# Feed-forward up-projection by seven quarter products, with buffers per sub-layer and the modulation sums moved

## The chip, the cores and the metric

The kernel runs on one core of a Trainium2 chip. The engines of a core each work through a queue of their own in order: TensorE (PE in the profile) multiplies matrices, VectorE (DVE), ScalarE (ACT) and GpSimd (POOL) work elementwise, and SyncE (SP) starts DMA transfers. They wait for one another through semaphores. The metric is the device time of one execution in microseconds (us).

## The reference

Two layers of a diffusion backbone run on 640 tokens (512 latent and 128 context) of 1024 channels. Each layer has a token mixer and then a feed-forward. Only the second is computed in another way by the change:

```python
def conv_glu(h, w_up, conv, w_down):
    u, val = jnp.split(h @ w_up, 2, axis=-1)     # 1024 -> 2 x 2816
    u = dwconv3(u, conv)                         # width 3, along the tokens
    return (jax.nn.gelu(u, approximate=True) * val) @ w_down

h = rmsnorm(x, g2n) * (1 + sc2) + sh2
x = x + gt2 * conv_glu(h, w_up, f_conv, w_down)
```

Shifts, scales and gates (`sh1, sc1, gt1, sh2, sc2, gt2`) come from `silu(c) @ w_mod + b_mod`, once for the latent tokens and once for the context tokens: 48 columns of 128 channels per layer.

## The kernel before

All matrices are float32. A product is made from three float32r products: weights and activations are each split into a high and a low part (`split`, L148 to L150, and in `block`, L127 and L128: ScalarE casts the high part, VectorE subtracts it to get the low part), and `gemm` (L136 to L147) sums high x high, high x low and low x high in PSUM. Channels lie on partitions. The 640 tokens are two halves of 320 columns (256 latent, 64 context), and a product tile of 128 channels is a pair of PSUM banks, one half in each. There are three such pairs (`mmps`, L102 to L109). A block of weights is 128 x 1024 (8 tiles of 128 channels) and needs 8 x 3 x 2 = 48 matmuls of 128x320.

`layer` (L648) runs a layer: norm, queries, keys and values, attention, pooling and short convolution, three branch projections (`branch`, 8 slots each, 24 in all), the output projection (`project`), the second norm (`norm`, one half of the tokens at a time, all from ready buffers) and `feed_forward` (L591). There, each of 22 channel tiles `f` has a gate block and a value block: 96 matmuls. ScalarE evacuates the gate product (L608), the convolution runs on ScalarE and VectorE (L293 to L295), ScalarE applies the GELU (L610), VectorE multiplies by the value product (L616) and the result is split. `PARTS` cuts the 22 tiles into two parts of 11; after each part `project` adds its share of the down-projection to `x`.

The modulation sums (`mod_block`, L162: two DMAs, four accumulating VectorE instructions and a small one for each of the 48 columns) are put behind other work by `aside`: in layer 0 one per branch slot (24), and two per tile of layer 0's feed-forward for the other 56.

Work is recorded in program order per engine and then ordered by a scheduler that sets each engine's queue and inserts the semaphore waits. All SBUF tiles come from pools that live for the whole kernel, so that the weights of the next stage can be fetched while the last one still runs.

Of the kernel before, what the change touches and what calls it, by code (L numbers as in the profile page):

```python
# [16 lines left out]
P = 128  # L17
D = 1024
# [19 lines left out]
KSPARE = (4, 4, 3)  # L38
FTAGS = [("yc", 8)] + [("g", 2)] * 2 + [("vm", 9)] * 9 + [("qk", 10)] * 10
# [6 lines left out]
PARTS = ((0, 11), (11, 22))  # L46
KSPLIT = (6, 5)
# [7 lines left out]
def hybrid_kernel(ctx: ExitStack, tc: tile.TileContext, a):  # L55
# [3 lines left out]
    wp = ctx.enter_context(tc.tile_pool(name="wp", bufs=1))  # L59
    act = ctx.enter_context(tc.tile_pool(name="act", bufs=1))  # L60
# [22 lines left out]

    count = [0]
# [3 lines left out]
    fturn = [0]  # L88
# [5 lines left out]

    def big(tag, bufs, dt=F32):
        return act.tile([P, N], dt, tag=tag, bufs=bufs, name=uid(tag))

    def tmp(dt=F32, width=N):
        t = act.tile([P, PPW], dt, tag="tmp", bufs=NTMP, name=uid("tmp"))
# [14 lines left out]
    def block(src, n=1024, spare=None):  # L114
        """spare: places (first column, end, tag and bufs of both parts) for when the rotating ones are all held."""
        raw = wp.tile([P, 1024], F32, tag="raw", bufs=NRAW, name=uid("raw"))
        nc.sync.dma_start(raw[:, :n], src)
        parts = []
        if spare is None:
            hi = wp.tile([P, 1024], F32R, tag="hi", bufs=NW, name=uid("hi"))  # L120
            lo = wp.tile([P, 1024], F32R, tag="lo", bufs=NW, name=uid("lo"))
            parts.append((0, n, hi, lo))
# [39 lines left out]
    def mod_block(l, i, cond):  # L162
        acc = sm.tile([P, 2, 2], F32, tag="macc", name=uid("macc"))
        for hf in range(2):
            turn[0] += 1
            tag, w = (("pt", 768), ("kc", 512), ("pt", 768), ("vca", 512))[turn[0] % 4]
            raw = act.tile([P, w], F32, tag=tag, bufs=2 if tag == "pt" else 1, name=uid("mraw"))[:, :512]
            nc.sync.dma_start(raw, a["w_mod"][l, i, :, hf * 512:(hf + 1) * 512])
            for s in range(2):
                scr = big("yt", 1)  # L170
# [25 lines left out]
    def rsqrt(st, v, r, t):  # L196
        """r = 1 / sqrt(st / D + EPS), with a Newton step"""
# [7 lines left out]
    def rstd(x, c, n=1):  # L205
        """1 / rms of the tokens of n halves from c on, the same on all partitions: one PSUM bank per half."""
# [17 lines left out]
    def half_tiles(n=2):  # L224
        t = act.tile([P, 768], F32, tag="pt", bufs=2, name=uid("xr"))
# [43 lines left out]
    def leading(n, src, h):  # L269
        """The first products after a norm: each half of the tokens for n blocks before the next half."""  # L270
# [95 lines left out]
    def softmax(s_ps, w, bias):  # L366
        s = act.tile([P, 384], F32, tag="s", bufs=4, name=uid("s"))
# [13 lines left out]
    def attention(l, qs, ks, vb, vc):  # L381
        kc = act.tile([P, 512], F32, tag="kc", bufs=1, name=uid("kc"))
        nc.sync.dma_start(kc, a["kc"][l].rearrange("p t n -> p (t n)"))
        vca = act.tile([P, 512], F32, tag="vca", bufs=1, name=uid("vca"))
# [4 lines left out]
        def behind(ins):  # L389
            """The products with V of the unit before: TensorE comes to them a little later than they could start."""  # L390
# [494 lines left out]
```

## Time and profile before

| | |
|---|---|
| three timed runs | 2156.16 us median (2154.4 to 2160.48) |
| span of the profiled execution | 2153.5 us (the page gives this execution by its span alone) |
| TensorE busy | 2114.8 us, 98% |
| VectorE busy | 1116.8 us, 52% |
| ScalarE busy | 723.3 us, 34% |
| GpSimd busy | 100.6 us, 5% |
| share of TensorE in the chain that ended last | 93% |
| HBM read | 216.10 MB, 103 GB/s over the span |

Busy times of TensorE include the overlap of pipelined matmuls: a matmul of 128x320 is shown with 310 ns, while the next one starts some 147 ns later. The granted TensorE clock is 1.00 (2.4 GHz) in nearly the whole span, and 0.50 (1.2 GHz) in a stretch near the start.

### The profile page before, as it was taken

The page shows a single profiled execution, that of the slowest core. Times are in us where ns is not written, and L with a number is a line of the kernel's source. Part 1 is how long each engine was busy: PE and PEld are TensorE (multiplying, and loading weights), DVE is VectorE, ACT ScalarE, POOL GpSimd, SP SyncE. Part 2 cuts the span into 40 slices and gives each one's busy share as a digit, 9 for nine tenths or more (in the row PEclk, how much of TensorE's full clock was granted, in tenths as well). Part 3 has the DMA queues.
Part 4 walks back from the last instruction along what each step waited for, and adds up shares of the span by engine and source line. Part 5 has one row for each costly group of instructions (what it writes and reads, how often), then busy time and mean ns, then how long its engine had stood idle before and what let it go on. Part 6 is the DMA issues. An engine that isn't in the chain of part 4 may idle for free.

```text
span 2153.5 us, 34873 instructions
## 1 busy us (share of the span) xinstructions
PE 2114.8 (98%) x14280; PEld 2038.5 (95%) x14280; DVE 1116.8 (52%) x2265; ACT 723.3 (34%) x1194; POOL 100.6 (5%) x300
## 2 busy tenths in 40 slices
PE   6999999999999999999999999999999999999998
PEld 4977999999999999999998779999999999999997
DVE  4247555556568778786352565323344643334434
ACT  4235432222354321333242452322223533123321
POOL 1001000000020000000020100000000200000000
PEclk9999999999999999999999999999999999999999
DMA  8241323345424445453322312222233222222222
GB/s 299 74 127 51 111 90 128 118 128 153 142 78 157 151 135 187 155 159 118 128 72 81 117 51 92 73 73 75 91 100 95 69 70 64 83 89 69 70 61 76
DMA packets 92032, 229.38 MB, mean 107 GB/s; under 512 B 10593, under 2 KB 20321, under 8 KB 91873
## 3 DMA queue, kind: packets, MB, share of 16 engines
q1 hardware_dynamic: 91872, 227.16, 33.4%
q8 instruction: 112, 1.84, 0.3%
q14 instruction: 48, 0.39, 0.1%
HBM read 216.10 MB, written 6.29 MB: 103 GB/s over the span
## 4 chain that ended last, share of the span: by engine, by line
PE 93%; DVE 3%; ACT 1%; POOL 1%; DMA 1%; issue 0%; SPq 0%; DVEq 0%; ACTq 0%; POOLq 0%
PE mm L141 60%; PE m L141 25%; PE ps L411 1%; PE ps L422 1%; PE m L401 1%; DVE h L150 1%; PE mm L346 1%; PE mm L344 1%; PE mm L345 1%; PE mm L732 1%; POOL xr L237 1%; POOL xr L234 0%; PE m L405 0%; DVE lo L128 0%; ACT h L149 0%
## 5 line engine op out<-in xcount | busy, mean ns | idle before, releaser
L141 PE MATMUL mm<-h,hi 128*128 128x320 f32 x3648 | 575.0, 310 | 1.0 <-ACT h L149 0.5
L141 PEld LDWEIGHTS mm<-h,hi 128*128 128x128 f32 x3648 | 542.2, 188 | 8.4 <-issue 2.1
L128 DVE TENSOR_TENSOR lo<-raw,hi 128x1024 fp32r<-128x1024 f32 (+1 forms) x240 | 278.8, 1162 | 367.8 <-PE mm L141 173.3
L127 ACT CAST hi<-raw 128x1024 fp32r<-128x1024 f32 (+1 forms) x240 | 240.5, 1003 | 585.0 <-PE mm L141 363.2
L141 PE MATMUL mm<-h,lo 128*128 128x320 f32 x1824 | 294.5, 310 | 0.0
L141 PEld LDWEIGHTS mm<-h,lo 128*128 128x128 f32 x1824 | 272.8, 188 | 3.4 <-issue 1.4
L171 DVE SCALAR_TENSOR_TENSOR yt<-mraw,cond 128x512 f32<-128x512 f32 x320 | 219.9, 687 | 5.4
L141 PE MATMUL m<-h,hi 128*128 128x320 f32 x1152 | 183.4, 311 | 4.1 <-ACT h L149 3.8
L141 PEld LDWEIGHTS m<-h,hi 128*128 128x128 f32 x1152 | 172.1, 188 | 8.7 <-ACT h L149 5.8
L128 DVE TENSOR_TENSOR yc<-raw,yc 128x512 fp32r<-128x512 f32 (+3 forms) x98 | 61.0, 624 | 130.0 <-ACT yc L127 72.8
L141 PE MATMUL mm<-vm,hi 128*128 128x320 f32 x626 | 113.1, 309 | 0.0
L141 PE MATMUL mm<-h,yc 128*128 128x320 f32 x672 | 100.9, 309 | 0.5 <-ACT tmp L608 0.5
L141 PE MATMUL m<-h,yc 128*128 128x320 f32 x672 | 100.9, 309 | 0.0
L141 PEld LDWEIGHTS mm<-h,yc 128*128 128x128 f32 x672 | 99.1, 188 | 0.7 <-ACT tmp L608 0.7
L141 PEld LDWEIGHTS m<-h,yc 128*128 128x128 f32 x672 | 99.1, 188 | 0.3 <-ACT tmp L608 0.3
L141 PEld LDWEIGHTS mm<-vm,hi 128*128 128x128 f32 x626 | 97.2, 188 | 0.4 <-DVE vm L150 0.4
L127 ACT CAST yc<-raw 128x512 fp32r<-128x512 f32 (+3 forms) x98 | 53.2, 565 | 130.0 <-DMA raw<-in_w_down 86.1
L141 PE MATMUL m<-h,lo 128*128 128x320 f32 x576 | 90.6, 308 | 0.0
L141 PEld LDWEIGHTS m<-h,lo 128*128 128x128 f32 x576 | 86.1, 188 | 0.0
L141 PE MATMUL mm<-yc,hi 128*128 128x320 f32 x370 | 75.4, 309 | 0.0
L141 PE MATMUL mm<-qk,hi 128*128 128x320 f32 x436 | 68.6, 309 | 0.0
L141 PEld LDWEIGHTS mm<-qk,hi 128*128 128x128 f32 x436 | 65.1, 188 | 0.0
(240 smaller groups left out, 2675.6 us busy)
## 6 DMA issues: line engine op xcount, KB each, us to landing
raw<-in_w_in SPq DMA_DIRECT2D x96, 512.0 KB, 3.6
raw<-in_w_up SPq DMA_DIRECT2D x88, 512.0 KB, 3.6
mraw<-in_w_mod SPq DMA_DIRECT2D x160, 256.0 KB, 2.9
raw<-in_w_branch SPq DMA_DIRECT2D x24, 512.0 KB, 3.5
raw<-in_w_down SPq DMA_DIRECT2D x30, 384.0 KB, 3.1
raw<-in_w_down SPq DMA_DIRECT2D x30, 320.0 KB, 2.9
raw<-in_w_out SPq DMA_DIRECT2D x16, 512.0 KB, 3.6
bm<-in_bias SPq DMA_DIRECT2D x16, 384.0 KB, 4.0
```

The costliest lines, as they stand in the source:

```text
L127: nc.scalar.copy(hi[:, :c1 - c0], raw[:, c0:c1])
L128: lows[0] = nc.vector.tensor_tensor(lo[:, :c1 - c0], raw[:, c0:c1], hi[:, :c1 - c0].bitcast(F32), ALU.subtract)
L141: nc.tensor.matmul(ps[:, c, :HALF], lhsT=w, rhs=v[:, c * HALF:(c + 1) * HALF], start=first, stop=last)
L150: return nc.vector.tensor_tensor(lo, src, hi.bitcast(F32), ALU.subtract)
L171: nc.vector.scalar_tensor_tensor(scr[:, :512], raw, 1.0, cond[s][:, hf * 512:(hf + 1) * 512], ALU.mult, ALU.mult, accum_out=acc[:, s, hf:h ...
L237: nc.gpsimd.tensor_scalar(t[:, HL:], t[:, HL:], sc[:, 1:2], sh[:, 1:2], ALU.mult, ALU.add)
L344: nc.tensor.matmul(o, lhsT=xh[:, tok], rhs=wh, start=(k == 0), stop=False)
L345: nc.tensor.matmul(o, lhsT=xh[:, tok], rhs=wl, start=False, stop=False)
L346: nc.tensor.matmul(o, lhsT=xl[:, tok], rhs=wh, start=False, stop=(k == KD - 1))
L401: nc.tensor.matmul(sps[:, e, 0:256].rearrange("p (r c) -> p r c", c=32), lhsT=qs[t][hs, j * P:(j + 1) * P], rhs=kb, start=True, stop=True)
L411: ins = nc.tensor.transpose(tp[:, b * P:(b + 1) * P], s[:, b * P:(b + 1) * P], ident)
L422: nc.tensor.matmul(y[e * 64:e * 64 + 64, 0:P], lhsT=v[:, t * P + e * 64:t * P + e * 64 + 64], rhs=pt[:, b, e, :], start=(b == 0), stop=(b ...
```

## The change

The two halves of the tokens and the two halves of the input channels make a 2 x 2 grid of `x`; gate and value columns with the two halves of the input channels make a 2 x 2 grid of the weights. Each tile `f` is then computed by seven products of sums of quarters (`seven`), each 12 matmuls of 128x320, or 84 for a tile. The sums of weight quarters are made on VectorE for each tile (`sums_block`), the sums of the norm's output once per sub-layer (`norm_quarters`). The first two products of a pair of banks start it, the later ones add to what the bank holds, and between them the bank is read: by ScalarE into a copy (`snap`) or by VectorE (`gate`, `val1`, `val0`). The gate product's evacuation moves to VectorE as the sum of the bank and a copy. The feed-forward has three parts (8, 8 and 6 tiles) instead of two.

SBUF tiles other than `x` and a few others now come from a pool per sub-layer (`Stage`), whose memory the next sub-layer's pool takes over. All modulation sums run in the branch slots: in layer 0 two per slot (48), in layer 1 up to two (32). The diff, cut to its core:

```diff
-PARTS = ((0, 11), (11, 22))
+PARTS = ((0, 8), (8, 16), (16, 22))
...
+    class Stage:
+        def __init__(self, name):
+            self.name = name
+            self.guard = tc.tile_pool(name=uid(name), bufs=1, reuse_waits="tile")
...
-                aside(ins, side, 1)
+                aside(ins, side, (len(side) + 23 - left[0]) // (24 - left[0]))
+                left[0] += 1
...
+    def split_quarters(out, t, ps):
+        n = 512 * len(ps)
+        hi, lo = own([P, 1024], F32R, "hi", 3, "hi"), own([P, 1024], F32R, "lo", 3, "lo")
+        split(t, hi[:, :n], lo[:, :n])
+        for j, p in enumerate(ps):
+            out[p] = (hi[:, j * 512:(j + 1) * 512], lo[:, j * 512:(j + 1) * 512])
+    def sums_block(raw, out):
+        if not out:
+            split_quarters(out, raw[:, 0:1024], (2, 1))
+        q = [raw[:, i * 512:(i + 1) * 512] for i in range(4)]
+        st = own([P, 2048], F32, "st", 1, "st")
+        s4, s3, s1, s2 = (st[:, i * 512:(i + 1) * 512] for i in range(4))
+        nc.vector.tensor_tensor(st[:, 512:1536].rearrange("p (b n) -> p b n", b=2),
+                                raw[:, 512:1536].rearrange("p (b n) -> p b n", b=2),
+                                q[3].unsqueeze(1).to_broadcast([P, 2, 512]), ALU.add)
+        nc.vector.tensor_tensor(s2, s1, q[1], ALU.add)
+        nc.vector.tensor_tensor(s4, s2, q[0], ALU.add)
+        for t, ps in ((st[:, 1024:2048], (5, 6)), (st[:, 0:1024], (3, 7)), (q[2], (4,))):
+            split_quarters(out, t, ps)
+        return out
+    def snap(src):
+        t = short("sn")
+        nc.scalar.copy(t, src)
+        return t
+    def seven(w, xt, ps, c11, c22, c12, c21):
+        a_, c_ = ps[:, 0, :HALF], ps[:, 1, :HALF]
+        kept = {}
+        def product(p, o, fresh):
+            for j, (wi, xi) in enumerate(((0, 0), (1, 0), (0, 1))):
+                for k in range(NP):
+                    nc.tensor.matmul(o, lhsT=w[p][wi][:, k * P:(k + 1) * P], rhs=xt[k][p][xi],
+                                     start=fresh and j == 0 and k == 0, stop=j == 2 and k == NP - 1,
+                                     skip_group_check=not fresh)
+        def one():
+            product(1, a_, True)
+            kept[1] = snap(a_)
+        def two():
+            product(2, c_, True)
+            c11(c_, kept[1])
+        def six():
+            product(6, a_, False)
+            kept[2] = snap(a_)
+        def five():
+            product(5, c_, True)
+            kept[5] = snap(c_)
+        def sev():
+            product(7, a_, False)
+            c22(a_, kept[5])
+        def three():
+            product(3, c_, False)
+            c12(c_, kept[2])
+        def four():
+            product(4, a_, False)
+            c21(a_)
+        return [one, two, six, five, sev, three, four]
...
+            nc.vector.tensor_tensor(x7, b22, b12, ALU.subtract)
+            nc.vector.scalar_tensor_tensor(x6, x7, -1.0, b11, ALU.mult, ALU.subtract)
+            two(u, i, 7, 6)
...
+                nc.vector.tensor_tensor(x5, b11, b12, ALU.subtract)
+                nc.vector.scalar_tensor_tensor(x4, x6, -1.0, b21, ALU.mult, ALU.subtract)
+                two(v, i, 5, 4)
...
+            def gate(c):
+                def do(psum, s):
+                    for (o, n), at in (((0, HL), LAT0 + c * HL), ((HL, HC), CTX0 + c * HC)):
+                        nc.vector.tensor_tensor(u[:, at:at + n], psum[:, o:o + n], s[:, o:o + n], ALU.add)
+                return do
+            def val1(psum, s):
+                got["v"] = short("v")
+                nc.vector.scalar_tensor_tensor(got["v"], psum, -1.0, s, ALU.mult, ALU.subtract)
+            def val0(psum):
+                cv = dwconv(u, "ffn_conv", l, f, KF)
+                nc.scalar.activation(cv[:, 1:PADW - 1], cv[:, 1:PADW - 1], AF.Gelu_apprx_tanh)
+                y = tmp()
+                for (o, n), at in (((0, HL), LAT0), ((HL, HC), CTX0)):
+                    nc.vector.scalar_tensor_tensor(y[:, o:o + n], psum[:, o:o + n], -1.0, cv[:, at:at + n],
+                                                   ALU.mult, ALU.mult)
+                for (o, n), at in (((0, HL), LAT0 + HL), ((HL, HC), CTX0 + HC)):
+                    nc.vector.tensor_tensor(y[:, HALF + o:HALF + o + n], got["v"][:, o:o + n], cv[:, at:at + n], ALU.mult)
+                got["y"] = y
+            return seven(w, xt, mmps(), gate(0), val1, gate(1), val0), got
```

In `up`, `gate(c)` is two VectorE sums from PSUM (256 and 64 columns, L752), `val1` one (320 columns, L757), and `val0` the convolution, the GELU and four VectorE products (L764, L767).

**TensorE, a tile of the feed-forward.** Before, in layer 1, a gate and a value block and the start of the next tile; `mm` and `m` are pairs of banks, `h` the norm's output, `hi`, `lo` and `yc` parts of the weights. Left out are rows without a wait.

```order
L141 MATMUL mm_17795<-h_16467,hi_17791 128x320 [waits DVE_49,PE_49,Activation_49]
...
L141 MATMUL mm_17795<-h_16467,lo_17792 128x320 [waits DVE_49]
...
L141 MATMUL mm_17861<-h_16467,hi_17857 128x320 [waits PE_49,Activation_49]
...
L141 MATMUL mm_17861<-h_16467,lo_17858 128x320 [waits DVE_49]
...
L141 MATMUL m_2785_17927<-h_16467,yc_17919 128x320 [waits DVE_49,PE_49]
```

Now, in layer 0, one tile (`mm_8158`) and the start of the next (`m_1427_8296`); `hT` are quarters of the norm's output and their sums. The rows shown start products 2, 6, 5 and 7, then product 1 of the next tile, its low part, products 3 and 4, and product 2 of the next tile.

```order
L653 MATMUL mm_8158<-hT_6301,hi_8134 128x320 [waits Activation_49]
...
L653 MATMUL mm_8158<-hT_6349,hi_8142 128x320 [waits DVE_49]
...
L653 MATMUL mm_8158<-hT_6370,hi_8142 128x320 [waits Activation_49]
...
L653 MATMUL mm_8158<-hT_6349,hi_8146 128x320 [waits Activation_49]
...
L653 MATMUL m_1427_8296<-hT_6301,hi_8272 128x320 [waits PE_49,Activation_49]
...
L653 MATMUL m_1427_8296<-hT_6301,lo_8273 128x320 [waits DVE_49]
...
L653 MATMUL mm_8158<-hT_6374,hi_8146 128x320 [waits DVE_49]
...
L653 MATMUL mm_8158<-hT_6370,hi_8150 128x320 [waits DVE_49]
...
L653 MATMUL m_1427_8296<-hT_6301,hi_8272 128x320 [waits Activation_49]
```

A block had waits at its start and at its low part. Now each product has one at its start: products 6, 3 and 4 for VectorE (by the semaphore counts for the end of `gate(0)`, `val1` and `gate(1)`), products 2, 5 and 7 for ScalarE (the three `snap`s). Each time that is the instruction which reads the product just before it, in the other bank of the pair. Product 1 of the next tile stands around product 3.

**VectorE, from one tile to the next.** Before, in the feed-forward of layer 1: `lo` and `yc` are weight parts for later blocks, `tmp` the convolution and the product, `vm`, `qk` the result's low part.

```order
L128 TENSOR_TENSOR lo_17598<-raw_17595,hi_17597 128x1024
L294 SCALAR_TENSOR_TENSOR tmp_17458<-tmp_17452,vecs,tmp_17458 128x642
L295 SCALAR_TENSOR_TENSOR tmp_17458<-tmp_17452,vecs,tmp_17458 128x642
L616 TENSOR_TENSOR tmp_17518<-mm_17469,tmp_17458 128x2x256
L616 TENSOR_TENSOR tmp_17518<-mm_17469,tmp_17458 128x2x64
L128 TENSOR_TENSOR lo_17660<-raw_17657,hi_17659 128x1024
L150 TENSOR_TENSOR qk_17522<-tmp_17518,qk_17521 128x640
L128 TENSOR_TENSOR yc_17728<-raw_17723,yc_17727 128x512
L128 TENSOR_TENSOR yc_17920<-raw_17917,yc_17919 128x512
L294 SCALAR_TENSOR_TENSOR tmp_17590<-tmp_17584,vecs,tmp_17590 128x642
```

Now, in layer 0, from the low part of products 5 and 6's weights for the next tile (`lo_8281`) to the end of that tile's `gate(0)` (both rows of `tmp_8292`):

```order
L171 TENSOR_TENSOR lo_8281<-st_8276,hi_8280 128x1024 [waits Activation_49]
L315 SCALAR_TENSOR_TENSOR tmp_8255<-tmp_8154,vecs,tmp_8255 128x642 [waits Activation_49]
L316 SCALAR_TENSOR_TENSOR tmp_8255<-tmp_8154,vecs,tmp_8255 128x642 [waits DVE_49,Pool_49]
L171 TENSOR_TENSOR lo_8285<-st_8276,hi_8284 128x1024 [waits Activation_49]
L764 SCALAR_TENSOR_TENSOR tmp_8260<-mm_8158,tmp_8255 128x256 [waits PE_49,Activation_49]
L764 SCALAR_TENSOR_TENSOR tmp_8260<-mm_8158,tmp_8255 128x64
L767 TENSOR_TENSOR tmp_8260<-v_8227,tmp_8255 128x256
L767 TENSOR_TENSOR tmp_8260<-v_8227,tmp_8255 128x64
L171 TENSOR_TENSOR lo_8289<-raw_8269,hi_8288 128x512 [waits Activation_49]
L752 TENSOR_TENSOR tmp_8292<-m_1427_8296,sn_8309 128x256 [waits PE_49]
L171 TENSOR_TENSOR gs_8266<-tmp_8260,gs_8265 128x640 [waits Activation_49]
L752 TENSOR_TENSOR tmp_8292<-m_1427_8296,sn_8309 128x64
```

The two L315 and L316 rows are the convolution, L764 and L767 `val0`, `gs_8266` the low part of the finished tile. The next tile's `gate(0)` has come to stand behind the convolution, two low parts of weights, `val0` and the low part of the result, and it is itself cut in two by the last of these.

**ScalarE at the same place, now.** `hi_8272`, `hi_8280`, `hi_8284` and `hi_8288` are the four high parts of the next tile's weights, `sn` the copies of banks, `tmp_8255` the convolution's middle tap and then the GELU.

```order
L170 CAST hi_8272<-raw_8269 128x1024 [waits DMAHW2_49,Activation_49]
L170 CAST hi_8280<-st_8276 128x1024 [waits DVE_49,PE_49,Activation_49]
L314 ACTIVATE tmp_8255<-tmp_8154,vecs 128x642 [waits DVE_49,Pool_49]
L641 COPY sn_8309<-m_1427_8296 128x320 [waits PE_49]
L170 CAST hi_8284<-st_8276 128x1024 [waits PE_49,Activation_49]
L761 ACTIVATE tmp_8255<-tmp_8255 128x642 [waits DVE_49]
L170 CAST hi_8288<-raw_8269 128x512 [waits DMAHW3_49,PE_49,Activation_49]
L170 CAST gs_8265<-tmp_8260 128x640 [waits DVE_49]
L641 COPY sn_8337<-m_1427_8296 128x320 [waits DVE_49,PE_49]
```

The three buffers of `hi` go round: `hi_8280` waits for TensorE to end product 3 of the tile before, `hi_8284` for product 4, and `hi_8288` for product 2 of its own tile. Before, the high parts had waits of the same kind, on blocks that had been multiplied earlier.

## Rows read from the trace of the kernel before

**Rows 1.** The page's busy times: engine, us, share of span, instructions.

```profile
PE 2114.8 (98%) x14280; PEld 2038.5 (95%) x14280; DVE 1116.8 (52%) x2265; ACT 723.3 (34%) x1194; POOL 100.6 (5%) x300
```

**Rows 2.** Busy time by stretch; the first row names the columns.

```profile
core 0: us, PE busy (x) PEld busy (x) DVE busy (x) ACT busy (x) POOL busy (x), PEclk, DMA share, GB/s
320.00:592.00 272.00, 272.00 (x1855) 271.81 (x1854) 160.83 (x317) 74.37 (x86) 0.00 (x0) 1.00 0.42 132
610.00:640.00 30.00, 28.31 (x179) 25.48 (x178) 23.03 (x55) 17.55 (x35) 14.14 (x27) 1.00 0.17 53
640.00:1086.00 446.00, 445.55 (x3038) 444.89 (x3038) 327.50 (x776) 143.02 (x225) 8.08 (x67) 1.00 0.46 146
1370.00:1640.00 270.00, 270.00 (x1841) 269.81 (x1841) 89.54 (x97) 71.24 (x83) 0.00 (x0) 1.00 0.28 85
1688.00:2136.00 448.00, 448.00 (x3055) 447.37 (x3055) 174.28 (x257) 144.42 (x226) 3.30 (x60) 1.00 0.23 71
```

**Rows 3.** The chain that ended last, inside the first feed-forward: start, us, what.

```profile
694.82 14.08 PE mm L141 x96
```

**Rows 4.** VectorE by line, operation and shape: count, busy us, mean ns, idle before.

```profile
L128 DVE TENSOR_TENSOR lo<-raw,hi 128x1024 fp32r<-128x1024 f32 x198 | 241.4, 1220 | 319.8 <-PE mm L141 142.4 <-PE m L141 70.5 <-issue 56.7
L128 DVE TENSOR_TENSOR yc<-raw,yc 128x512 fp32r<-128x512 f32 x78 | 53.6, 690 | 109.5 <-ACT yc L127 72.8 <-PE mm L141 14.2 <-ACT hi L127 10.1
L295 DVE SCALAR_TENSOR_TENSOR tmp<-tmp,vecs,tmp 128x642 f32<-128x642 f32 x52 | 47.6, 916 | 2.2
L294 DVE SCALAR_TENSOR_TENSOR tmp<-tmp,vecs,tmp 128x642 f32<-128x642 f32 x52 | 45.9, 884 | 15.9 <-ACT tmp L293 15.7
L230 DVE TENSOR_TENSOR xr<-ps,mx 128x320 f32<-128x320 f32 x48 | 22.1, 480 | 0.7 <-PE ps L219 0.6
L150 DVE TENSOR_TENSOR vm<-tmp,vm 128x640 fp32r<-128x640 f32 x24 | 19.7, 820 | 4.6 <-ACT vm L149 4.6
L616 DVE TENSOR_TENSOR tmp<-mm,tmp 128x512 f32<-128x512 f32 x30 | 20.7, 689 | 66.7 <-PE mm L141 66.7
L616 DVE TENSOR_TENSOR tmp<-mm,tmp 128x128 f32<-128x128 f32 x30 | 8.4, 280 | 0.0
L562 DVE SCALAR_TENSOR_TENSOR mx<-mm,mod,mx 128x256 f32<-128x256 f32 x14 | 6.7, 481 | 11.4 <-PE mm L141 11.3
L562 DVE SCALAR_TENSOR_TENSOR mx<-mm,mod,mx 128x64 f32<-128x64 f32 x14 | 3.8, 274 | 0.0
```

**Rows 5.** ScalarE in the same view.

```profile
L127 ACT CAST hi<-raw 128x1024 fp32r<-128x1024 f32 x198 | 207.6, 1050 | 511.9 <-PE mm L141 320.0 <-PE m L141 140.5 <-PE mm L346 18.1
L127 ACT CAST yc<-raw 128x512 fp32r<-128x512 f32 x78 | 46.7, 617 | 122.4 <-DMA raw<-in_w_down 86.1 <-DMA raw<-in_w_up 34.9 <-PE mm L141 1.3
L293 ACT ACTIVATE tmp<-tmp,vecs 128x642 f32<-128x642 f32 x52 | 43.3, 833 | 16.4 <-DVE tmp L476 11.2 <-issue 2.2
L610 ACT ACTIVATE tmp<-tmp 128x642 f32<-128x642 f32 x44 | 32.6, 741 | 89.6 <-DVE tmp L295 89.6
L608 ACT COPY tmp<-mm 128x512 f32<-128x512 f32 x28 | 16.4, 588 | 50.6 <-PE mm L141 50.5
L608 ACT COPY tmp<-mm 128x128 f32<-128x128 f32 x28 | 7.6, 271 | 0.0
```

**Rows 6.** The timeline of a branch slot: start, us, engine, what, idle before.

```profile
340.75 2.36 PE L141 MATMUL mm<-h,lo 128*128 128x320 f32 x15
343.14 0.71 ACT L540 ACTIVATE g<-mm 128x640 f32<-128x640 f32 x1 [1.29 <-PE mm L141]
```

**Rows 7.** Busy time by stretch near the start; columns as in Rows 2.

```profile
28.00:32.00 4.00, 1.26 (x6) 0.61 (x5) 2.77 (x4) 2.83 (x6) 0.00 (x0) 0.97 1.05 386
32.00:36.00 4.00, 4.00 (x17) 4.00 (x18) 4.00 (x9) 0.58 (x1) 0.52 (x1) 0.50 1.05 388
36.00:40.00 4.00, 4.00 (x21) 4.00 (x21) 1.85 (x4) 1.69 (x3) 2.42 (x3) 0.67 1.04 406
56.00:60.00 4.00, 2.37 (x16) 2.11 (x15) 4.00 (x2) 0.00 (x0) 2.72 (x2) 1.00 0.00 0
```

More of the change, by code (lines that the diff above doesn't have):

```diff
@@ L87, in hybrid_kernel @@
     busy = [False]
-    fturn = [0]
     lows = [None]
@@ L119, in block @@
         if spare is None:
[L120 to L122 removed]
+            parts.append((0, n, own([P, 1024], F32R, "hi", NW, "hi"), own([P, 1024], F32R, "lo", NW, "lo")))
         else:
@@ L526, in aside, with branch @@
         del side[:n]
-    def branch(l, b, h, ys, merged, last=False, side=[], between=None):
+    def branch(l, b, h, ys, merged, left, last=False, side=[], between=None):
         parts = []
@@ L570, in project @@
             gemm(ps, get(m), xt)
-            aside(residual(l, x, ps, m, part), side, 2)
+            aside(residual(l, x, ps, m, part), side, 1)
         if n_last:
@@ L620, in feed_forward @@
-                gs.append((gh, gl))
-                aside(ins, side, 2 if f < f1 - 1 else 0)
-            def wdown(m, i=0):
-                out = []
-                k0 = f0
-                spare = iter([("yc", 8)] * 6)
-                for n in KSPARE if i else KSPLIT:
-                    places = [(0, n * P, next(spare), next(spare))] if i else None
-                    src = a["w_down"][l, m, :, k0 * P:(k0 + n) * P]
-                    blk = block(src, n * P, places) if f1 == KF and m >= KD - 2 else ffn_block(src, n * P)
-                    out += [cols(blk, k) for k in range(n)]
-                    k0 += n
-                return out
@@ L635, in feed_forward @@
-            assert f1 < KF or not side
-            rb = project(l, x, wdown, 5, gs, 2 if f1 == KF else 0, side)
+                    steps, got = lead[f]
+                    sums_block(raws[0] if f == 0 else load_quarters(a["w_up"][l, f]), ws[f])
+                else:
+                    steps, got = up(f)
+                for step in steps:
+                    step()
+                gs.append(finish(got))
+            n = f1 - f0
+            last = f1 == KF
+            raws = {}
+            def wdown(m, i=0):
+                if m % 2 == 0 or not raws:
+                    raws["t"] = own([P, 2048], F32, "raw", 2, "raw")
+                raw = raws["t"][:, m % 2 * 1024:m % 2 * 1024 + n * P]
+                nc.sync.dma_start(raw, a["w_down"][l, m, :, f0 * P:f1 * P])
+                hi, lo = own([P, 1024], F32R, "hi", 3, "hi"), own([P, 1024], F32R, "lo", 3, "lo")
+                split(raw, hi[:, :n * P], lo[:, :n * P])
+                return [cols([(0, n * P, hi, lo)], k) for k in range(n)]
@@ L637, in feed_forward @@
+            rb = project(l, x, wdown, 5, gs, 2 if last else 0)
         return rb
@@ L646, in mods, with mixer @@
         return [do(i) for i in idx]
-    def layer(l, x, rb):
+    def mixer(l, x, rb):
         if l == 0:
```

200 lines of the change are left out of this document (129 added, 71 removed).

## The prediction

> **What bounds the kernel now.** I read the page's busy times first: TensorE works 98% of the span, the others half of it or less [rows 1]. Then the busy times by stretch: in both feed-forwards (640 to 1086 us, 1688 to 2136 us) and in the branch stages TensorE has no gap, while VectorE is 73% busy in layer 0's feed-forward, which carries modulation sums, and 39% in layer 1's, which carries none [rows 2]. So TensorE's matmuls set the end, and their price is their spacing. The chain of waits shows 96 of them in 14.08 us, 0.1467 us each [rows 3]: a tile of the feed-forward (a gate and a value block) takes 14.08 us.
>
> **What the change removes.** A tile needs 84 matmuls instead of 96. Over 22 tiles and 2 layers that is 528 x 0.1467 = 77.4 us less. If TensorE stayed without gaps, a tile would take 12.32 us.
>
> **What it adds to a tile.** TensorE will not stay without gaps. In the built order each product has a wait at its start for the instruction that reads the product before it, although that one lies in the other bank of the pair. So the products of a tile do not run beside their evacuations; they alternate with them. The only other work for TensorE is product 1 of the next tile around product 3, and product 2 after product 4. I follow one tile round, from the start of product 6 to that of the next tile's.
>
> A product takes 11 x 0.147 plus 0.31 for its last matmul (the last of 15 in 2.36 us [rows 6]), 1.92 us. A `snap` of 320 columns lies between the PSUM copies of 128 and 512 columns, 0.271 and 0.588 us: 0.43 [rows 5]. `val1` is like a VectorE operation on 320 columns from PSUM, 0.48; `gate` has 256 and 64 columns, by the line through 0.280 (128) and 0.689 (512) 0.416 and 0.212; `val0` has two scalar operations (0.481, 0.274) and two plain ones (0.416, 0.212), 1.38 [rows 4].
>
> - From product 6 to the end of product 3: product 6 1.92, snap 0.43, product 5 1.92, snap 0.43. ScalarE then casts the next tile's first high part (1.05), VectorE makes its low part (1.22) and only then `val1` (0.48), which is queued behind it; product 7 (1.92) runs beside the first two of these. Then product 3, 1.92. Sum 9.37 us.
> - From there to the next product 6, all on VectorE but the first: the high part for products 5 and 6, whose buffer product 3 has just freed, 1.05; its low part 1.22; the convolution 0.884 + 0.916; the low part for products 3 and 7 1.22; `val0` 1.38; the last low part 0.69; `gate(0)` 0.416 + 0.212, with the finished tile's low part, 0.82, between them. Sum 8.81 us. `gate(1)`, the middle tap (0.833), product 4, the GELU (0.741) and the other casts (0.617, 0.728) lie beside that.
>
> The round is 18.2 us. Handing over costs little (ScalarE starts 0.03 us after the last matmul ends [rows 6]), and queued VectorE instructions overlap a little; I let the two cancel. TensorE works 12.3 of these 18.2 us and waits 5.9, of which about 4.0 in one piece: product 4 starts some 0.75 us after product 3's end, products 4 and 2 take 3.5 and the tail, product 6 comes at 8.8. Apart from the first three tiles 19 tiles per layer go round like this: 38 x 5.9 = +224 us. I allow the round 1 us less or 0.7 more: -38 or +27.
>
> The clock adds to it. Near the start TensorE was busy 1.26 of 4 us, after which the granted clock was 0.50 (1.2 GHz) for the next 4 and part of the 4 after that, some 7 us, though TensorE was then busy throughout; a stretch with 2.37 of 4 us busy was followed by no fall [rows 7]. The new gap lies between: 4.0 us without a matmul, but dense work before it. If the clock fell there, product 6 and most of product 5 would run at half speed, 10 + 8 matmuls' worth of 0.147 us more: 2.7 us per tile. I take half, 38 x 1.35 = +51, between 0 and +103.
>
> The Trainium skill, "TensorE: Matmul & The Clock Gate", section "HAM oscillation — how this bites in real kernels", says that a loop whose matmuls wait in every pass falls back to the low clock in every pass and pays for it each time. By that rule the clock term would be the whole +103; the rows above show one such fall after a sparse stretch and none after a shorter one.
>
> **The start of a feed-forward.** Before, the second norm was hidden: 28.31 of 30 us busy at 610 to 640 [rows 2]. Now VectorE must do, between the last output projection and the first product 6, 39 operations of 320 columns (0.49), 12 of 640 (0.82), 4 low parts of 1024 (1.22), the first sums (1.22 + 0.69 + 0.69) and six gate operations (1.9), 38 us; less what queued ones overlap, about 34. TensorE has 72 matmuls meanwhile, 10.6 us, and the first weights land only after the last output block, whose buffers they take over. Idle 23, before 1.7: +22 us, and +4 for the three leading tiles, whose VectorE work is a little over TensorE's. For two layers +52, between +20 and +80.
>
> **The other edits.** Layer 0's branch slots get a second modulation sum. Layer 0's branch stage has 71 us more VectorE work than layer 1's for 24 sums [rows 2], 3.0 us a sum; a slot of 72 matmuls is 10.56 us, and VectorE would be busy (160.83 + 71) of 272, 85%. Their DMAs go through SyncE's queue as before, and the low part of a block is needed only 32 matmuls into it, 4.7 us. Cost 0, hidden by these; 1 us a slot, 24, if that cover fails. Taking the sums out of the feed-forward gains nothing by itself, since TensorE had no gap there. The second mixer's pool takes memory from the feed-forward, so its weights and norm come late: +5, between 0 and +10. The third part and the down-projection (the same matmuls): 0, between -6 and +12.
>
> **Sum.** -77 + 224 + 51 + 52 + 5 = +255 on the span of 2153.5: 2408. The median of the runs shown stands 2.7 above that span: 2411 us.
>
> **Rivals.**
> - *The clock falls in every tile.* For it: 4 us without any matmul. Against: the fall that the trace shows came after a sparser time before it. +52 on the forecast: 2462. Were the half clock to stay for longer than 7 us, still more.
> - *It never falls.* The spell with 2.37 of 4 us busy speaks for it. 2411 - 51 = 2360.
> - *Waits by bank.* Matmuls run on in one bank while the other is read, as the products are arranged. Then VectorE decides: per tile 4.35 (low parts) + 2.60 (sums) + 1.80 + 1.26 + 0.48 + 1.38 + 0.82 = 12.7 us, and about 1.3 in which it must wait for product 3, 14.0. 38 x 1.7 = 65; -77 + 65 + 52 + 5 = +45: 2201. Against: the waits stand in the built order.
> - *Faster: TensorE stays the bound.* If VectorE's work of a tile came below 12.32 us and lay beside the products, only the start of the feed-forward would be lost: -77 + 52 + 5 = -20, 2136. It decides from 12.32 us of VectorE work downwards; the rows give 12.7, and the waits speak against it too.
>
> The page "PSUM — Partial Sum Buffer" of the Trainium skill, section "PSUM bank collisions raise a hardware error", says to guard PSUM with semaphores by bank, not by address. By it the third rival would be the natural build; the order shows waits that reach across the two banks of a tile, so what the rule permits is not what is built.
>
> **How the numbers follow.** Chances: forecast 0.56, clock falls always 0.20, never 0.18, waits by bank 0.04, faster 0.02. The waits are in the program and the durations are measured, so hardly anything is left on the fast side; about 0.3% (6 us) is what a measurement of this kernel can tell from no change. Low end: the clock never falls (-51), and a round 1 us shorter (-38), or part of that with a cheaper start: 2315. High end: it falls always (+52), a longer round (+27), a dearer start or branch stage (+28): 2520. Faster 0.02, same 0.01, slower 0.97.
>
> **What would show it.** Right: TensorE busy about 90% or less of the span; in the feed-forwards a repeat of some 18 to 21 us per tile, with TensorE's longest idle before product 6 and ended by VectorE's `gate` line; VectorE busy some 70% there; granted clock below 1.00 in the feed-forwards. The step on the waits is wrong if product 6 runs while `gate(0)` reads; the clock step if the clock is 1.00 throughout or 0.50 in most tiles; the start if the first product 6 comes less than 25 us after the output projection; the branch step if TensorE has gaps in layer 0's slots. The forecast falls if the tile's period is 14 us or less.

## The result and the profile after

The changed kernel takes 2454.73 us (median; 2445.22 to 2461.77) against 2157.32 for the kernel before (2154.4 to 2160.48): 1.138 times as long (95% interval 1.135 to 1.142), +297 us. The forecast was 2411, with a range of 2315 to 2520. The profiled executions span 2443.4 and 2153.5 us, +289.9; the budget below goes by these.

From the page of the kernel after: the engines, and TensorE's granted clock in 40 slices of the span (a 9 is 0.90 or more).

```profile
PE 2175.4 (89%) x13752; PEld 2051.0 (84%) x13752; DVE 1406.6 (58%) x2791; ACT 804.3 (33%) x1261; POOL 114.0 (5%) x300
PEclk9999999999788988998999999999988899889889
```

The 528 matmuls are gone (14280 before [rows 1], now 13752), yet TensorE is busy 60.6 us longer, and idle 268.0 us where it was idle 38.7. Only the two feed-forwards have slices in which the clock is below 0.90. What TensorE waited for, from the list of its waits (who waits, for what, us in total, times, longest):

```profile
PE mm L653 <- DVE tmp L752: 83.0, 25, 3.7
PE m L653 <- DVE tmp L752: 44.8, 13, 3.7
PE mm L653 <- ACT sn L641: 29.8, 58, 0.5
PE mm L653 <- ACT hi L170: 22.2, 4, 15.7
PE m L653 <- ACT hi L170: 21.1, 2, 15.6
PE m L653 <- ACT sn L641: 15.4, 30, 0.5
```

L653 is the matmul of `seven`. It waits for `gate` (L752) 25 + 13 = 38 times, 127.8 us; for a `snap` (L641) 88 times, two per tile, 45.2 us; and at the starts of the feed-forwards for high parts of the weights (L170), 43.3 us. The longest of these, 15.7 us per start, is for the high part of the first weight sums, which VectorE makes only behind its work on the norm. Busy times by stretch (columns as in [rows 2]): the branch stage of layer 0, the start of the first feed-forward, and 80 us of the second:

```profile
320.00:592.00 272.00, 271.46 (x1849) 270.94 (x1849) 224.75 (x535) 70.83 (x83) 0.17 (x3) 1.00 0.52 171
618.00:660.00 42.00, 17.74 (x86) 15.69 (x86) 35.97 (x75) 20.33 (x35) 19.44 (x24) 0.67 0.17 60
...
2080.00:2160.00 80.00, 61.66 (x330) 57.37 (x329) 45.89 (x76) 26.27 (x38) 0.66 (x12) 0.84 0.15 53
```

In the branch stage VectorE took 64 us more work than in [rows 2] and TensorE still has no gap. In the feed-forward no engine is full: TensorE 77%, VectorE 57%. That is the mark of engines that take turns. One turn, in TensorE's timeline (start, us of the group; in brackets the idle time before it and what ended it):

```profile
2149.66 0.75 PE L653 MATMUL mm<-hT,hi 128*128 128x320 f32 x4
2154.10 0.96 PE L653 MATMUL mm<-hT,hi 128*128 128x320 f32 x4 [3.69 <-DVE tmp L752]
...
2164.68 0.75 PE L653 MATMUL mm<-hT,hi 128*128 128x320 f32 x4
...
2174.71 1.08 PE L653 MATMUL m<-hT,hi 128*128 128x320 f32 x4 [3.68 <-DVE tmp L752]
```

These four rows are the end of product 2, product 6, product 3 and the next tile's product 6: a round of 20.61 us, 10.58 of it up to product 3 and 10.03 from there.

VectorE in that gap:

```profile
2150.09 1.22 DVE L171 TENSOR_TENSOR lo<-st,hi 128x1024 fp32r<-128x1024 f32 x1
2151.22 0.55 DVE L764 SCALAR_TENSOR_TENSOR tmp<-mm,tmp 128x256 f32<-128x256 f32 x2
2151.68 0.55 DVE L767 TENSOR_TENSOR tmp<-v,tmp 128x256 f32<-128x256 f32 x2
2152.15 0.69 DVE L171 TENSOR_TENSOR lo<-raw,hi 128x512 fp32r<-128x512 f32 x1
2152.75 0.42 DVE L752 TENSOR_TENSOR tmp<-mm,sn 128x256 f32<-128x256 f32 x1
2153.09 0.82 DVE L171 TENSOR_TENSOR gs<-tmp,gs 128x640 fp32r<-128x640 f32 x1
2153.82 0.22 DVE L752 TENSOR_TENSOR tmp<-mm,sn 128x64 f32<-128x64 f32 x1
```

Product 2 ends at 2150.41. Its two `gate` instructions take 0.64 us, but they stand behind a low part, `val0` and another low part, with a third low part between them; only then may product 6 start, in the other bank. The same gap by the clock, in windows of 4 us:

```profile
2146.00:2150.00 4.00, 4.00 (x28) 3.82 (x28) 3.30 (x5) 3.14 (x4) 0.00 (x0) 1.00 0.01 2
2150.00:2154.00 4.00, 0.41 (x3) 0.15 (x1) 4.00 (x11) 1.97 (x3) 0.17 (x3) 1.00 0.04 10
2154.00:2158.00 4.00, 3.39 (x13) 2.99 (x14) 2.56 (x4) 0.42 (x1) 0.00 (x0) 0.58 0.72 254
2158.00:2162.00 4.00, 3.49 (x13) 3.09 (x13) 0.00 (x0) 0.69 (x2) 0.00 (x0) 0.56 0.00 0
```

A 4 us gap, and the next 8 us pass at about half the clock: 13 matmuls where 27 or 28 fit. The fall isn't as long in every round: in the 28 rounds that run from one long gap to the next, the stretch from product 6 to product 3 takes 9.2 to 13.0 us, 10.44 on average, and the rest of the round always about 10.04.

### The profile page after: what moved, and what is told of

The parts are those of the page before. It is cut to its first block, busy times and chain, and to the rows that moved or that the text cites. A ratio compares the mean times of both kernels' runs of the same rounds, so it can differ in the third digit from the quotient of the medians.

```text
span 2443.4 us, 34349 instructions
## 1 busy us (share of the span) xinstructions
PE 2175.4 (89%) x13752; PEld 2051.0 (84%) x13752; DVE 1406.6 (58%) x2791; ACT 804.3 (33%) x1261; POOL 114.0 (5%) x300
## 5 line engine op out<-in xcount | busy, mean ns | idle before, releaser
L653 PE MATMUL mm<-hT,hi 128*128 128x320 f32 x1624 | 353.7, 348 | 138.4 <-DVE tmp L752 83.0
L653 PEld LDWEIGHTS mm<-hT,hi 128*128 128x128 f32 x1624 | 286.7, 214 | 172.2 <-DVE tmp L752 93.5
L162 PE MATMUL mm<-h,hi 128*128 128x320 f32 x2336 | 375.6, 314 | 8.5 <-ACT hi L148 5.9
L162 PEld LDWEIGHTS mm<-h,hi 128*128 128x128 f32 x2336 | 350.4, 190 | 16.3 <-ACT hi L148 6.1
L171 DVE TENSOR_TENSOR lo<-raw,hi 128x1024 fp32r<-128x1024 f32 (+2 forms) x136 | 138.4, 1018 | 225.3 <-ACT hi L170 225.3
L653 PE MATMUL m<-hT,hi 128*128 128x320 f32 x840 | 186.5, 348 | 84.6 <-DVE tmp L752 44.8
L149 DVE TENSOR_TENSOR lo<-raw,hi 128x1024 fp32r<-128x1024 f32 x140 | 170.8, 1221 | 141.2 <-PE mm L162 60.6
L653 PEld LDWEIGHTS m<-hT,hi 128*128 128x128 f32 x840 | 148.8, 214 | 102.7 <-DVE tmp L752 50.3
L170 ACT CAST hi<-raw 128x1024 fp32r<-128x1024 f32 (+2 forms) x136 | 119.7, 880 | 176.4 <-PE mm L162 89.5
L653 PE MATMUL mm<-hT,lo 128*128 128x320 f32 x812 | 177.0, 341 | 0.0
L170 ACT CAST hi<-st 128x1024 fp32r<-128x1024 f32 x88 | 92.1, 1049 | 228.6 <-issue 131.0
L653 PEld LDWEIGHTS mm<-hT,lo 128*128 128x128 f32 x812 | 147.2, 215 | 0.2 <-DVE lo L171 0.2
L162 PE MATMUL mm<-gs,hi 128*128 128x320 f32 x936 | 147.3, 310 | 0.0
L171 DVE TENSOR_TENSOR lo<-st,hi 128x1024 fp32r<-128x1024 f32 x88 | 107.4, 1222 | 24.9 <-ACT hi L170 24.9
L641 ACT COPY sn<-mm 128x320 f32<-128x320 f32 x87 | 36.5, 419 | 197.6 <-PE mm L653 197.6
```

The costliest lines, as they stand in the source:

```text
L149: lows[0] = nc.vector.tensor_tensor(lo[:, :c1 - c0], raw[:, c0:c1], hi[:, :c1 - c0].bitcast(F32), ALU.subtract)
L162: nc.tensor.matmul(ps[:, c, :HALF], lhsT=w, rhs=v[:, c * HALF:(c + 1) * HALF], start=first, stop=last)
L170: nc.scalar.copy(hi, src)
L171: return nc.vector.tensor_tensor(lo, src, hi.bitcast(F32), ALU.subtract)
L641: nc.scalar.copy(t, src)
L653: nc.tensor.matmul(o, lhsT=w[p][wi][:, k * P:(k + 1) * P], rhs=xt[k][p][xi], start=fresh and j == 0 and k == 0, stop=j == 2 and k == NP - ...
```

## The experiments

Theory: the loss is (a) waits that reach across the two banks of a tile, so that products and evacuations alternate, and (b) a clock that falls in the gap this opens. Rivals: VectorE simply has too much work (the weight sums); the weight buffers come free too late; the modulation sums cost something. Ratios are to the kernel before on the same chip, with a 95% interval.

### One bank per tile

The up-projection's pair becomes two tiles of one bank each, so that no wait can reach across:

```diff
-        a_, c_ = ps[:, 0, :HALF], ps[:, 1, :HALF]
+        a_, c_ = ps[0][:, :HALF], ps[1][:, :HALF]
...
-            return seven(w, xt, mmps(), gate(0), val1, gate(1), val0), got
+            ps = [pairs[-1].tile([P, 512], F32, tag=t, bufs=3, name=uid(t)) for t in ("ma", "mc")]
+            return seven(w, xt, ps, gate(0), val1, gate(1), val0), got
```

> The two halves of the PSUM pair that a tile of the up projection uses are two separate one-bank tiles; the rest is the same. In the built order product 6 then waits for the snap of product 1 alone, product 7 for that of product 6, and product 5, now behind product 7, for gate(0). Theory (the waits across the two banks make the idle time): products run beside evacuations, VectorE's own work of about 12.7 us a tile decides, a round of about 14.2 us instead of the 20.0 of the changed kernel's trace, TensorE waits about 1.9 us a tile in short gaps, the granted clock stays near 1.00: 2445 - 38 x 5.8 = 2225 us (2195 to 2260). Rival (the queue of VectorE decides whatever the banks): round 17.5 us or more, 2360 or above. Rival (the waits for weight buffers decide): the same 19 to 20 us, no change.

2227.56 us, 1.035 (1.033 to 1.036): 227 us of the 297 are gone by this edit alone. Its waits, and 60 us of its first feed-forward:

```profile
PE ma L656 <- ACT sn L644: 20.7, 34, 1.1
PE mc L656 <- ACT sn L644: 14.4, 28, 0.5
PE mm L165 <- DVE tmp L767: 8.4, 2, 4.2
```

```profile
860.00:920.00 60.00, 55.74 (x366) 53.37 (x364) 49.29 (x84) 29.80 (x45) 0.73 (x15) 1.00 0.21 71
```

No wait for `gate` is left, and the clock is 1.00. The last line is a price of this build: its banks change hands at each part.

### The gap filled

The kernel after, with 20 matmuls into a bank that nobody reads, put behind product 2:

```diff
...
-            product(2, c_, True)
+            last = product(2, c_, True)
+            with tc.issue_after(last.ins):
+                idle = smps()
+                for j in range(20):
+                    nc.tensor.matmul(idle[:, :HALF], lhsT=w[2][0][:, j % NP * P:(j % NP + 1) * P], rhs=xt[j % NP][2][0],
+                                     start=True, stop=True)
```

> Behind product 2 of every tile 20 more matmuls of 320 columns go into a PSUM bank that nothing reads (2.9 us of work in the gap of 3.7 us before product 6). Nothing else waits for them. Theory (the half clock after the gap costs about 2.3 us of every round): the granted clock is 1.00 in the steady tiles, the round 17.7 us, 2445 - 38 x 2.3 = 2357 us (2340 to 2380). Rival (the clock falls for another reason, or the 2.3 us are lost elsewhere): within 0.5% of 2450. Rival (added matmuls delay product 6): slower than 2450.

2343.55 us, 1.088 (1.086 to 1.089). TensorE does 880 more matmuls and the kernel is 109 us faster (1.1382 less 1.0877, of 2155):

```profile
2080.00:2160.00 80.00, 76.91 (x512) 74.69 (x511) 42.87 (x68) 26.04 (x34) 0.49 (x9) 1.00 0.25 80
...
878.68 0.75 PE L653 MATMUL m<-hT,hi 128*128 128x320 f32 x4
...
886.54 0.75 PE L653 MATMUL m<-hT,hi 128*128 128x320 f32 x4
...
895.67 0.75 PE L653 MATMUL mm<-hT,hi 128*128 128x320 f32 x4
...
894.64 0.55 DVE L758 TENSOR_TENSOR tmp<-mm,sn 128x256 f32<-128x256 f32 x2
...
896.24 0.82 DVE L171 TENSOR_TENSOR gs<-tmp,gs 128x640 fp32r<-128x640 f32 x1
```

The clock is 1.00, and a round (product 6, product 3, the next product 6) takes 16.99 us instead of 20.5. The time is the one expected, but the round is 0.7 us shorter than the expected 17.7, because the edit did two things. From product 6 to product 3 the round takes 7.86 us instead of 10.44: these 2.58 us are the clock. From product 3 to the next product 6 it takes 9.13 us instead of 10.04, and that is VectorE's order: in this build both `gate(0)` additions (L758) stand ahead of the finished tile's low part (L171 `gs`) and the last low part of the weights, one of which stood between them and the other ahead of them in the kernel after. With 34 long gaps the clock's share is about 34 x 2.58 = 88 us of the 109.

### Gate first

The kernel after, `gate` ahead of VectorE's other ready work (the addition itself, the same but for its indent, is left out):

```diff
-                    for (o, n), at in (((0, HL), LAT0 + c * HL), ((HL, HC), CTX0 + c * HC)):
+                    with tc.high_priority():
+                        for (o, n), at in (((0, HL), LAT0 + c * HL), ((HL, HC), CTX0 + c * HC)):
...
```

> The additions that gate(0) and gate(1) make stand ahead in VectorE's order: gate(0) now after the first of val0's four operations instead of behind all four, the last low part and the finished tile's low part. Theory (the long gap is VectorE's queue in front of gate(0)): the gap before product 6 falls from 3.7 to about 1.3 us; then the clock need not fall either: a round of 15.3 us, 2445 - 38 x 4.7 = 2266 us; 17.6 us and 2355 if the clock falls all the same. Rival (the weight buffers decide): what gate(0) gains the next low part loses, round above 19 us, 2420 or more.

2336.16 us, 1.085 (1.082 to 1.089). Its waits for `gate`, and two stretches of its tiles:

```profile
PE mm L653 <- DVE tmp L753: 41.9, 25, 2.6
...
PE m L653 <- DVE tmp L753: 22.5, 13, 2.6
...
840.00:900.00 60.00, 49.42 (x312) 45.47 (x311) 40.65 (x66) 23.58 (x35) 0.50 (x9) 1.00 0.21 71
900.00:960.00 60.00, 49.41 (x296) 45.70 (x295) 39.83 (x68) 25.12 (x36) 0.49 (x9) 0.94 0.17 54
```

The 38 waits take 64.4 us, 1.7 each, instead of 127.8. That is 63 of the 115 us gained (1.1382 less 1.085, of 2155); the other 52 would be a good half of the clock's 88. The clock stays up in some stretches and falls in others. Neither expectation had that, and the time lies between them.

### Weight buffers

Part 4's high and low parts in buffers of their own (`own([P, 512], F32R, "h4", 1, "h4")` and `"l4"` in `split_quarters`), so that the next tile's casts need not wait for product 3.

> The high and low part of quarter 4 have buffers of their own, so the three rotating pairs serve three parts of a tile instead of four (the short tiles are 5 instead of 6). Theory (evacuations across the banks and VectorE's queue decide, not weight buffers): the round without the clock's loss stays 17.7 to 18.2 us, but product 1 of the next tile now comes between product 4 and product 6, so the gap before product 6 is in pieces of 0.8 to 1.7 us. With no fall of the clock this gives 2445 - 38 x 2.0 = 2370 us, with one 2450. Rival (the weight buffers decide): round 15 us or less, 2250 or below.

2370.98 us, 1.101 (1.099 to 1.104).

```profile
860.00:920.00 60.00, 45.11 (x257) 40.53 (x256) 36.90 (x61) 22.90 (x32) 0.49 (x9) 0.94 0.16 53
```

The gap is broken into pieces of up to 1.49 us here, the clock stays higher, but in this stretch TensorE is idle about as much as before. The kernel is 80 us faster than the kernel after (1.1382 less 1.1011, of 2155), close to the 2370 expected without a fall, though the clock still fell in part; its steady round is 18.1 us, where the rival had 15 or less. The waits remain: the weight buffers are not what holds the round at this length.

### One bank per tile throughout, and the sums left out

The next kernel lets the down-projection use the one-bank tiles too, so that no bank changes hands within a feed-forward. The one after it leaves out the sums as well.

> As e1_banks, but the down projection too works on the one-bank tiles (its residual then in four instructions instead of two), so that no PSUM pool changes hands between a part's last tile and its down projection; in e1_banks' trace TensorE waited 4.2 us at such a place. Theory: six such places per run, 6 x 4 = 24 us less than e1_banks: 2204 us (2195 to 2215). Rival (that wait is for the last tile's own result, which product k = 7 needs in any case): 2222 to 2230.

2199.74 us, 1.021 (1.019 to 1.022), as expected: banks that change hands had cost some 28 us. Its products 6, 7 and the next 6:

```profile
859.32 0.85 PE L666 MATMUL ma<-hT,hi 128*128 128x320 f32 x4 [0.52 <-ACT sn L654]
...
863.62 0.85 PE L666 MATMUL mc<-hT,hi 128*128 128x320 f32 x4 [0.52 <-ACT sn L654]
...
873.19 0.85 PE L666 MATMUL ma<-hT,hi 128*128 128x320 f32 x4 [0.52 <-ACT sn L654]
```

A round is 13.87 us: my third rival, waits by bank, had 14.0 and 2201 us. That its numbers fit so well is luck, for it gave VectorE's load as the reason, which the next kernel refutes. "PSUM — Partial Sum Buffer" of the Trainium skill, section "PSUM bank collisions raise a hardware error", which wants guards by bank, agrees with these two kernels; the kernel after guards by tile.

```diff
...
-        for t, ps in ((st[:, 1024:2048], (5, 6)), (st[:, 0:1024], (3, 7)), (q[2], (4,))):
+        for t, ps in ((raw[:, 1024:2048], (5, 6)), (raw[:, 0:1024], (3, 7)), (q[2], (4,))):
```

> As e5_singles, with the three weight sums of VectorE left out (2.6 us a tile); the products take the loaded quarters instead, so the output is not the reference's. Theory (with the banks apart VectorE's work decides the round): e1_banks has rounds of 13.7 us with TensorE busy 92%, without the sums VectorE has 10.1 us a tile against TensorE's 12.3, round 12.6, 44 x 1.1 = 48 us less than e5_singles: about 2156 us (2140 to 2175). Rival (the chain of waits between products decides, not VectorE's load): within 10 us of e5_singles.

2186.15 us, 1.014 (1.012 to 1.015). Missed: 13.6 us less, where 48 were expected (25 to 60 by the range) and the rival had 10 at most.

```profile
870.28 0.85 PE L659 MATMUL ma<-hT,hi 128*128 128x320 f32 x4 [1.05 <-ACT sn L647]
...
883.92 0.85 PE L659 MATMUL ma<-hT,hi 128*128 128x320 f32 x4 [1.05 <-ACT sn L647]
```

With 2.60 us less VectorE work per tile the round is 13.64 instead of 13.87, and the wait left is for a `snap`. So VectorE's load is not what sets the round. The place of an evacuation between two products of one bank is left; the kernel with `gate` first, below, tests that.

### The sums on GpSimd

The same kernel (sums kept), with the three sums as `nc.gpsimd.tensor_tensor`; and a second one that in `norm_quarters` also makes the operands of products 3, 4 and 5 after all those of 6 and 7.

> As e5_singles, with the three weight sums on GpSimd instead of VectorE. Theory (VectorE's load decides, and GpSimd has time: 2048 columns of sums in a round of 12.6 us): like e6_nosum, about 2160 us (2140 to 2185). Rival (GpSimd is too slow, or its work beside VectorE's slows both): slower than e5_singles, 2210 or more.

> As e7_gpsums, and at the start of the feed-forward the operands of products 3, 4 and 5 are made behind those of products 6 and 7 of all four pairs, instead of after every second pair. Theory (VectorE's norm and sums before the first product 6 make the 15.7 us in which TensorE stands): two pairs' rest, 2 x 2.3 = 4.6 us, moves behind the first product 6, 9 us less than e7_gpsums over two layers. Rival (products 5 and 3 of the leading tiles then wait for the same work): no difference to e7_gpsums.

2307.2 us, 1.071 (1.069 to 1.073), and 2307.25, 1.070 (1.069 to 1.072). Both missed; the times are those of the rivals. GpSimd's first sum of one tile, and TensorE's row:

```profile
879.78 2.92 POOL L643 TENSOR_TENSOR st<-raw 128x1024 f32<-128x1024 f32 x1 [10.74 <-DVE lo L177]
...
868.35 1.44 PE L666 MATMUL ma<-hT,hi 128*128 128x320 f32 x4 [3.00 <-ACT sn L654]
...
860.00:920.00 60.00, 48.02 (x291) 46.97 (x290) 43.21 (x59) 24.62 (x37) 24.25 (x24) 0.91 0.16 54
```

With the two sums of 512 columns (1.33 and 1.74 us) this is 5.99 us instead of 2.60, and the sums start only when the low part of the sums before them has been read, since `st` has one buffer: a chain of sums, cast and low part from tile to tile. A 3.0 us gap opens, and the clock falls (0.91). That this chain sets the 17 us is argued from the release of the first sum, not tested with a second buffer. The order of the operands makes no difference.

### Gate first, one bank per tile

The kernel with one bank per tile throughout (1.021), and `gate` under priority as above.

> As e5_singles, with the gate additions put ahead in VectorE's order as in e3_gate. In the built order the products then alternate between the two banks (6, 5, 7, 3, 4); in e5_singles 7 stands behind 6 and 3 behind 5 in the same bank, and its trace shows 0.52 us of waiting for a snap at each of the two, a round of 13.87 us. Theory (chain of snaps, not VectorE's load, holds the rest): the two waits go, round 12.4 us, 38 x 1.45 = 55 us less than e5_singles: 2145 us (2130 to 2165), faster than the kernel before by about 0.5%. Rival (VectorE's load of some 11.5 us a tile already decides): round above 13.3 us, 2178 or more.

2161.26 us, 1.003 (1.002 to 1.004). Start and steady part of its first feed-forward:

```profile
620.00:664.00 44.00, 17.65 (x93) 15.83 (x91) 36.50 (x75) 21.11 (x36) 18.11 (x24) 0.71 0.18 62
664.00:1060.00 396.00, 395.16 (x2652) 390.77 (x2652) 286.33 (x501) 173.11 (x239) 3.38 (x60) 0.99 0.26 85
860.00:920.00 60.00, 59.79 (x402) 58.65 (x401) 48.96 (x84) 32.77 (x46) 0.82 (x15) 1.00 0.27 89
```

The time is in the expected range; that the kernel would beat the one before was missed. TensorE now has hardly a gap in 396 us, and a round is 12.65 us. The products alternate banks in the built order (6, 5, 7, 3, 4), so each evacuation lies beside a product of the other bank. VectorE works 286 of 396 us, and 48.96 of 60 us in the tiles alone, where the down-projection doesn't thin it out; so it is near the pace there without setting it. What is left of the loss is mainly the start: 17.65 of 44 us busy, where the kernel before had 41.97:

```profile
620.00:664.00 44.00, 41.97 (x271) 39.41 (x271) 29.32 (x62) 23.91 (x42) 11.11 (x27) 1.00 0.28 90
```

### The start of a feed-forward

Two steps from there. First: the first tile's sums under priority ahead of the norm, and the operands of 3, 4 and 5 last.

> As e9_gatefirst, and at the start of the feed-forward the first tile's weight sums stand ahead, and the operands of products 3, 4 and 5 come behind those of products 6 and 7. Theory (VectorE has some 35 us of work before the first product 6 and its amount decides, not its order): the gap before the first product 6 shrinks by 2 us or less of its 18, most is made up for by waits of the leading tiles: 0 to 6 us less than e9_gatefirst. Rival (only the order holds product 6 back): 10 us or more less over two layers.

2155.55 us, 1.0003 (0.9994 to 1.0012), 5.7 less than the kernel it starts from, as expected. One of its waits at the start:

```profile
649.93 0.63 PE L666 MATMUL ma<-hT,hi 128*128 128x320 f32 x1 [4.22 <-ACT hT L176]
```

Product 6 starts earlier (649.93 instead of 662.98), but crawls from operand to operand as the norm delivers them, with further waits of 3.68 and 3.06 us. Second: the scaling of the norm from GpSimd to ScalarE, `x5` to GpSimd, and the next mixer's first weights ahead of the stores of `x` in SyncE's queue.

> As e10_start, with two edits at different places. At the second mixer's start the first three weight loads stand ahead of the eight stores of the residual stream in SyncE's queue; before, each store waited there for its residual, and the first load went out 2 us before the first product was due. In the norm of the feed-forward the latent half of all channel tiles is scaled on ScalarE (half of them were on GpSimd), and x5 is subtracted on GpSimd instead of VectorE. Theory (the loads wait behind the stores, not for memory): the gap of 5.9 us before the second mixer's first product falls to some 2 us; the start of each feed-forward gains 1 to 3 us: 6 to 10 us less than e10_start, 2148 us (2143 to 2153), faster than the kernel before by 0.2 to 0.5%. Rival (the loads wait for memory of the feed-forward, or the first product waits for the norm): gap 5 us or more, no difference to e10_start.

2154.0 us, 0.9996 (0.9987 to 1.0005): the same as before, and the 6 to 10 us expected are missed. The weights were asked for at 1047.93, but the wait at the second mixer's start stayed at 5.87 us:

```profile
1047.93 1.45 SPq L146 DMA_DIRECT2D raw<-in_w_in  x3
...
1084.92 0.47 ACT L215 ACTIVATE sq<-mx 128x320 f32<-128x320 f32 x1
1085.29 1.03 ACT L154 CAST hi<-raw 128x1024 fp32r<-128x1024 f32 x1
...
1086.38 1.17 PE L169 MATMUL m<-h,hi 128*128 128x320 f32 x3 [5.87 <-ACT hi L154]
```

ScalarE comes to the cast (L154) only after the squares of the norm (L215). So neither the loads' place in SyncE's queue nor memory holds the first product, since they were asked for 37 us earlier. Of the rival's two reasons the norm is left: the weights' cast stands behind it in ScalarE's queue.

### The modulation sums alone

The kernel before, with the sums moved as in the change (`aside` with up to two per slot, none in the feed-forward).

> The kernel before with one part of the change alone: the modulation sums of the feed-forwards stand in the branch stage (two a slot in layer 0, 32 in layer 1). Theory (hidden on both sides): the same as before within 0.3%. Rivals: 24 us slower, 1.1%, if every slot of layer 0 loses 1 us; 6 us faster or more if the sums delayed something in the feed-forward.

2157.06 us, 1.0007 (0.9998 to 1.0016).

```profile
320.00:592.00 272.00, 271.46 (x1850) 270.94 (x1848) 225.02 (x532) 71.02 (x83) 5.51 (x4) 1.00 0.59 178
```

The moved sums cost nothing, as in the kernel after.

## Why the prediction was right, and which step was not

- **Matmuls removed, -77.** Right: 528 fewer, and where nothing waits they are a gain (hardly a gap in 396 us with `gate` first).
- **The products alternate with their evacuations, +224.** Right in mechanism: a wait before product 6 in 38 rounds, ended by `gate`, long in 34 of them (up to 3.69 us; forecast about 4.0) and 0.77 in the first round of each later part. That the waits reach across banks is shown by the one-bank kernel, where they vanish. Measured: 127.8 us in these waits, 38 x 1.04 in the two `snap` waits, and four product tails of 0.16, 38 x 0.65: 192, 32 less. VectorE is 57% busy, not the 70% I named.
- **The clock: the mis-sized term.** "I take half, 38 x 1.35 = +51" is the step that failed. A price of 2.7 us per fall was right (2.58 on average, by the filled gap), but the clock fell in all 28 rounds measured, not in half: some 34 x 2.58 = 88 us. The dense work before a gap does not protect: in the windows above the 4 us before it are 4.00 busy. What I held against the fall, the sparser time before the one in [rows 7], was no argument. "TensorE: Matmul & The Clock Gate" of the Trainium skill, section "HAM oscillation — how this bites in real kernels", had a fall in every pass of such a loop; the trace agrees (+103 by that rule, some 88 measured, with 34 long gaps instead of 38). Deviation +37.
- **The start, +52.** Low. From the end of the output projection to the first product 6 it is 41.6 us (618.04 to 659.62; 41.5 in layer 1), not 34. Two early gaps (5.41 and 1.59) and the clock (0.67 there) belong to it. About +15 for both layers.
- **The second mixer, +5.** The stage takes 591.45 us instead of 579.5, +12; its first products wait 5.87 us for weights, 1.16 for a low part of weights and 1.16 for the norm's output. Deviation +7.
- **The modulation sums, 0.** Right, shown by the kernel that has this edit alone.

Together: -32 + 37 + 15 + 7 = +27, where the spans are +34.9 above the forecast (289.9 against 255). The first mixer and output projection end at 618.04 us, 617.64 before, so the other 8 must lie in the feed-forwards: in the leading tiles, the slow stretch behind the start and the ends of the parts, which I didn't take apart.

Of the rivals, "the clock falls in every tile" (2462) is what happened; I gave it 0.20 against 0.56 for the half-way case. That it comes within 7 us is partly luck: its waits and its clock are some 32 and 15 us too high, and the start and the second mixer together 22 too low. "Faster: TensorE stays the bound" came true for the tile loop of the kernel with one-bank tiles and `gate` first, though not for the whole time. There 77 us of matmuls are saved and the total is 6 us above before, so some 83 us are lost elsewhere; the stretch 620:664 shows 24 of them for one layer (41.97 less 17.65 busy), with VectorE 36.50 of 44 us busy on the norm and its sums, which nothing hides. That the amount of this work is the cause is argued: reordering it gained 5.7 us and no more. I found no version that beats the kernel before.

## What to carry to other kernels

Look at what the waits guard, not at what the algorithm needs: with two accumulators in one tile, a reader of one blocked the writer of the other in this build, and separate tiles gave back 227 of 297 us. An evacuation that releases the busiest engine goes to the head of its engine's queue, and a gap of a few us in every pass is priced with the slow stretch behind it. Work that is removed from a loop is worth only what the start of that loop does not take back.

## What was not expected of the hardware

The clock's answer to gaps is steep: rounds with a 3.69 us gap lost 1.3 to 5.1 us each to the clock (in the one shown, 8 us ran at 0.56 to 0.58); with gaps of 3.0 us a stretch of 60 us ran at 0.91, with gaps of 1.7 us one at 1.00 and the next, where one gap was 2.3, at 0.94; waits of 0.52 us, two a round, left it at 1.00. More matmuls made the kernel faster: 20 useless ones in each of 44 tiles, 109 us, most of it the clock. The same 128x1024 float32 addition takes 2.92 us on GpSimd and 1.22 on VectorE.
